# Attention in units of one kv group: 512-column logit matmuls, value products in runs of up to eight key blocks, sums in the values' array form

## The chip, the cores and the metric

The kernel runs on one core of one Trainium2 chip. What is compared is the device time of one launch in microseconds (us). The core has a matrix engine (PE, with its weight loads shown as PEld), a vector engine (DVE), an activation engine (ACT), GpSimd (POOL), and a queue engine (SP) that issues DMA transfers. Each takes its instructions in a fixed order, and they meet at semaphores.

## The reference, cut to what matters

One layer over 4096 tokens of width 1024. An indexer picks up to 256 keys for each query; attention runs over these, with 8 query heads in 2 kv groups of 4 heads, and head width 64. A second branch pools over windows; gates merge both.

```
qg = qb.reshape(B, Q_BLOCK, N_KV_A, rep, HEAD_DIM)        # rep = 4 heads share a kv group
s = jnp.einsum('bqgrd,bqkgd->bqgrk', qg, kg) * scale
s = jnp.where(valid[:, :, None, None, :], s, -jnp.inf)
p = jax.nn.softmax(s, axis=-1)
o = jnp.einsum('bqgrk,bqkgd->bqgrd', p, vg)
...
y = g[:, :, 0] * (a @ w_branch_a[layer]) + g[:, :, 1] * (b @ w_branch_b[layer])
x = x + y @ w_out[layer]
```

The kernel doesn't gather keys. It computes dense causal attention in blocks of 128 queries by 128 keys, and adds a bias of -1e30 to the keys left out.

## The kernel before

Four stages follow one another: the input projection, the indexer with the gates, `phase_attention`, and `phase_out` (the merge and the last projection). In the profiled execution attention begins at about 2110 us and ends at about 3697 us.

`phase_attention` works on query block b = 0..31 in two units, so there are 64. A unit of before holds a "half": two heads of each of the two kv groups. It goes through key blocks kt = 0..b, 1056 in all over the 64 units. The steps of a unit are these.

- `maxima` (L1278 to L1319): for each of its 4 heads the logits with the queries in the partitions (L1296, up to 512 keys a matmul), then a reduction on DVE with the bias (L1302) in pieces of up to 1024 keys, each taking the maximum of the piece before as a scalar from memory. The 4 maxima are turned by a matmul with 4 weight columns (L1311) and written by ACT (L1317) into rows 64 to 67 of `ql`.
- logits again with the keys in the partitions (`logits`, L1337): for each kv group a product of `ks` with `qh` and one of `k2` with `ql` (L1342, L1343), 256 columns each, so four matmuls to a key block, which fill one PSUM bank `st`. DVE adds the turned bias (L1354), and ACT takes the exponential (L1357) into a tile `tt` of two key blocks.
- value products (`values`, L1366): 64 weight columns a group, one group to each half of the array, 256 columns. They are fp32, and each becomes two instructions, so a key block is four instructions. `PVN = 2`: they are issued when two key blocks are there.
- POOL adds up the `tt` tiles (L1382); `sums` (L1396) multiplies the total by 32 columns of ones, in four places of the array. The sums are turned (L1190), inverted on DVE (L1412, L1413), turned again (L1418), copied by ACT (L1420) and stored in `invD`. The unnormalised output goes through `ov` to `oD`.

The rings: `st` has 3 PSUM banks (`SB = 3`) and serves the logits, all transpositions, the turned bias and the sums; `ps` has 2 tiles of two banks for `maxima`; `pv` has one bank. `tt` has 7 tiles, `sm` two.

The order of the instructions is made by `Plan.run`, a model of the engines: each engine takes the ready step of the least key whose new tiles have room. A step is issued whole. The key of a value step is that of its last block plus `LAG`. All DMAs go through SP in that order.

During the last unit the weights of `phase_out` are loaded, `w_branch_a` and then `w_branch_b`, each in 8 pieces of 512 columns through a ring `raw` of two; ACT and DVE split each piece into two parts (L252, L254). `phase_out` starts with branch b.

Of the kernel before, what the change touches and what calls it, by code (L numbers as in the profile page):

```python
# [12 lines left out]
F32 = mybir.dt.float32  # L13
# [13 lines left out]
CH = 512  # L27
# [11 lines left out]
LAG = 6  # L39
SB = 3  # L40
LAT = 0.1
TB = 7
FL = 8
FB = 0
# [19 lines left out]
BS = 0  # L64
# [6 lines left out]
PVN = 2  # L71
# [27 lines left out]
ORDN = 0  # L99


def ORD(n):
    r = list(range(n))
    k = ORDN % 100
    if ORDN < 100:
        return r[k:] + r[:k][::-1]
    if ORDN < 200:
        return r[k:-1] + r[:k][::-1] + r[-1:]
    small, big = r[:k], r[k:]
    out = []  # L110
    while big:
        out.append(big.pop(0))
        if small and len(out) > 2:
            out.append(small.pop())
    return out + small


# [4 lines left out]
class Tile_:  # L122
    """A tile of a plan: its ring, and the steps that use it."""
# [108 lines left out]
class Weights:  # L232
    """The two parts of a matrix [n * P, D], put there by steps of a plan with a ring "raw"."""

    def __init__(self, k, pl, name, n, queue):
        self.k, self.pl, self.name, self.n, self.queue, self.parts, self.steps = k, pl, name, n, queue, [], []

    def put(self, k, key, rows, pool, after=()):
        nc, pl = self.k.nc, self.pl
        for c in range(0, D, CH):  # L240
            raw = pl.new("raw")
            cs = slice(c, c + CH)
# [15 lines left out]
class K:  # L258
# [6 lines left out]
    def consts(self):  # L265
# [13 lines left out]
        self.cst = cp.tile([P, a["cst"].shape[1]], F32, name="cst")  # L279
# [4 lines left out]
    def tables(self, pt):  # L284
        """Small parameters, transposed or spread over the partitions, and the sines and cosines."""
# [50 lines left out]
    def rsqrt(self, pool, v, shape):  # L336
        """v <- 1 / sqrt(v), with one Newton step."""
# [10 lines left out]
    def mm3(self, out, lh, ll, rh, rl, kt):  # L348
        """out = sum over k of (lh + ll)[k]^T (rh + rl)[k] without the product of the two low parts."""
# [6 lines left out]
    def phase1(self):  # L356
# [5 lines left out]
        with ExitStack() as es:  # L362
# [8 lines left out]
            def ep():  # L371
                """The last x is used: its place goes to the first weights and tokens of the next phase."""
# [175 lines left out]
    def on_early(self, part):  # L548
        """What the next phase reads first."""
# [10 lines left out]
    def load_h(self, pool, c, w, bufs):  # L560
        """hi and lo of the transposed normed input, [P, w/128, KT, P], for tokens c*w .. (c+1)*w."""
# [16 lines left out]
    def guess(self, pl, new, ring, key):  # L578
        """A first threshold per row, and how far to look: the scores taken as independent normal heads."""
# [58 lines left out]
    def phase_index(self):  # L638
        """Scores of the indexer, the 256 greatest of each row, and the bias of the keys left out;
        between them the projections of the gates, of z_a and of branch b up to its own projection."""  # L640
# [40 lines left out]
        def span(i):  # L681
            """Time of a slot: the scores of one group and the search of the one before."""
# [13 lines left out]
        # the last tile's key of the indexer  # L696
# [27 lines left out]
        def prep(b, key):  # L724
            """The queries of block b, transposed, four times each: hi, hi, lo, lo."""
# [21 lines left out]
        def scores(b, key, total, free):  # L747
            """The scores of block b, added to what tells equal ones apart."""
# [166 lines left out]
        # the search  # L915
# [21 lines left out]
    def dense(self, pl, new, rp):  # L937
# [19 lines left out]
        def pool(c, g, t, pu, pz, done):  # L957
            """Trailing means of u less u, and silu(z)."""
# [56 lines left out]
        def weight(s, m, kind, i, t):  # L1015
            """The two parts of a block of weights."""
# [131 lines left out]
    def phase_attention(self):  # L1148
        """Attention over the keys that are left. The logits come twice: once with the queries in the
        partitions and the keys in full, the queries' high part, for the maximum of a row, and once with  # L1150
        the keys in the partitions, in full and less that maximum, for the exponentials, which then
        need no transposition before their product with the values."""
        nc, tc, a = self.nc, self.tc, self.a
        self.oD = self.dp.tile([4, P, S], F32, name="oD")
        self.invD = self.dp.tile([8, S], F32, name="invD")
# [4 lines left out]
        v, act, pe = nc.vector, nc.scalar, nc.tensor  # L1160
        ks = sp.tile([P, 2, S], F32R, name="ks")
        k2 = sp.tile([P, 2, S], F32R, name="k2")
# [6 lines left out]
        sel = self.cst[:, 96 + 8 * NB:96 + 8 * NB + 4]  # L1169
# [151 lines left out]
        def softmax(u):  # L1321
# [6 lines left out]
            for kt in range(b + 1):  # L1328
# [8 lines left out]
                def logits(s=s, kt=kt, on=on):  # L1337
                    o = slice(kt * P, (kt + 1) * P)
                    for g in range(2):
# [4 lines left out]
                        if on:  # L1344
                            pe.matmul(out, id4, bc(bt.t[:, kt:kt + 1], [P, 2, P]), start=False, stop=True)
# [282 lines left out]
```

## Time and profile before

| | us |
|---|---|
| median of 3 runs | 4449.38 (4447.02 to 4452.2) |
| span of the profiled execution | 4442.4 |
| attention in it, about | 2110 to 3697 |
| PE busy in the span | 4312.9 (97%) |
| DVE busy in the span | 3328.8 (75%) |
| POOL busy in the span | 1884.9 (42%) |

The median lies 7 us above the span of the profiled execution, which begins at its first instruction and ends at its last. In the page, PE's busy time includes the tail of each matmul, which overlaps the next one; how much room PE has is read from the chain of work that ended last, where each piece has only the time by which it moved the end.

### The profile page before, as it was taken

The numbers are of one execution on the slowest core, as the hardware profiler recorded it, in microseconds if no ns is written. First come the engines' busy times: TensorE is split into PE (matmuls) and PEld (weight loads), VectorE is DVE, ScalarE is ACT, GpSimd is POOL, SyncE is SP. The second block draws the span as 40 slices with busy tenths as digits, with TensorE's granted clock in tenths as the row PEclk, the third lists the DMA queues.
The fourth block names the chain that finished last, engine by engine and source line by source line (L and its number), as shares of the span: only waits on it lengthen the run. The fifth ranks groups of instructions, "written<-read, shape, count | busy, mean of one in ns | idle before, by whom it ended". The sixth has DMA issues, their size and how long they took to land.

```text
span 4442.4 us, 82747 instructions
## 1 busy us (share of the span) xinstructions
PE 4312.9 (97%) x30890; PEld 3656.7 (82%) x30891; DVE 3328.8 (75%) x7933; ACT 2391.8 (54%) x4057; POOL 1884.9 (42%) x1775
## 2 busy tenths in 40 slices
PE   8999999999999999998999999999999998999999
PEld 7998999999998989998666666666666766899998
DVE  5444798999999888896788888888898985343432
ACT  4332786786877778875655555555555553111110
POOL 3555223224334330100356777777777882111111
PEclk9999999999999999999999999999999999999999
DMA  6444445445444456655321111110100005554542
GB/s 204 173 162 155 162 155 183 156 154 183 154 167 153 154 175 200 211 194 175 77 65 40 35 30 32 33 25 27 26 27 19 13 17 169 155 148 137 147 137 86
DMA packets 390912, 523.57 MB, mean 118 GB/s; under 512 B 118189, under 2 KB 294633, under 8 KB 390378
## 3 DMA queue, kind: packets, MB, share of 16 engines
q1 hardware_dynamic: 390506, 518.24, 36.0%
q8 instruction: 244, 4.00, 0.4%
q14 instruction: 162, 1.33, 0.1%
HBM read 374.32 MB, written 143.82 MB: 117 GB/s over the span
## 4 chain that ended last, share of the span: by engine, by line
PE 50%; DVE 1%; DMA 1%; ACT 0%; issue 0%; SPq 0%; POOL 0%; DVEq 0%; ACTq 0%; POOLq 0%
PE pv L1369 12%; PE st L1342 7%; PE ps L1296 6%; PE st L1343 6%; PE po L1522 3%; PE po L1523 3%; PE po L1524 3%; PE pa L1524 3%; PE pa L1523 2%; PE pa L1522 2%; PE st L1190 1%; PE st L1402 1%; PE st L1270 1%; PE st L1311 0%; DMA ga<-gD 0%
## 5 line engine op out<-in xcount | busy, mean ns | idle before, releaser
L1059 PE MATMUL pd<-h,wgh 128*128 128x256 f32 x3584 | 1017.1, 284 | 8.9 <-ACT row L427 8.9
L1382 POOL TENSOR_TENSOR acc<-acc,tt 128x1024 f32<-128x1024 f32 x388 | 925.7, 2386 | 201.7 <-ACT tt L1357 180.6
L1060 PE MATMUL pd<-h,wgh 128*128 128x256 f32 x3584 | 1010.1, 282 | 0.0
L1061 PE MATMUL pd<-h,wgl 128*128 128x256 f32 x3584 | 1009.6, 282 | 0.0
L1357 ACT ACTIVATE tt<-tt 128x512 f32<-128x512 f32 x1056 | 646.3, 628 | 406.5 <-DVE tt L1354 403.2
L1354 DVE TENSOR_TENSOR tt<-st,bT 128x512 f32<-128x512 f32 x1056 | 703.4, 685 | 139.5 <-PE st L1343 127.6
L777 DVE SCALAR_TENSOR_TENSOR ring<-rl,wi,ring 128x1024 f32<-128x1024 f32 (+7 forms) x624 | 699.3, 1161 | 9.3 <-ACT rl L775 6.0
L1059 PEld LDWEIGHTS pd<-h,wgh 128*128 128x128 f32 x3584 | 682.2, 190 | 27.9 <-ACT row L427 9.2
L1060 PEld LDWEIGHTS pd<-h,wgh 128*128 128x128 f32 x3584 | 682.6, 190 | 14.5
L1061 PEld LDWEIGHTS pd<-h,wgl 128*128 128x128 f32 x3584 | 682.0, 190 | 0.0
L775 ACT ACTIVATE rl<-ps 128x1024 f32<-128x1024 f32 (+7 forms) x624 | 538.1, 888 | 133.6 <-PE ps L772 55.0
L1342 PE MATMUL st<-qh,ks 128*128 128x256 f32 x2112 | 593.5, 307 | 4.8 <-DVE tt L1354 2.9
L1369 PE MATMUL pv<-tt,vv 128*64 128x256 f32 x4224 | 573.8, 392 | 0.0
L1343 PE MATMUL st<-ql,k 68*128 68x256 f32 x2112 | 544.0, 283 | 0.4 <-ACT ql L1317 0.4
L1342 PEld LDWEIGHTS st<-qh,ks 128*128 128x128 f32 x2112 | 400.3, 190 | 158.2 <-issue 59.6
L862 ACT ACTIVATE sg<-ring,tk 128x2048 fp8e4<-128x2048 f32 (+8 forms) x322 | 485.4, 1509 | 39.4 <-DVE tk L849 19.6
L1343 PEld LDWEIGHTS st<-ql,k 68*128 68x128 f32 x2112 | 401.4, 190 | 11.5 <-ACT ql L1317 0.7
L1369 PEld LDWEIGHTS pv<-tt,vv 128*64 128x64 f32 x4224 | 255.8, 136 | 179.8 <-issue 49.3
L1302 DVE CUSTOM_DVE_ANT_0 jk<-ps,bias,mx 128x1024 bf16<-128x1024 f32 (+7 forms) x384 | 399.9, 1041 | 2.9 <-PE ps L1296 1.8
L1296 PE MATMUL ps<-ks,qh 128*128 128x512 f32 (+3 forms) x1152 | 372.9, 399 | 2.2 <-DVE mf L1302 1.1
L1555 POOL TENSOR_TENSOR ga<-ga,gb 128x256 f32<-128x256 f32 x128 | 103.9, 821 | 634.4 <-DVE gb L1550 370.9
L772 PE MATMUL ps<-kis,qT 128*128 128x512 f32 (+3 forms) x1136 | 340.1, 388 | 15.0 <-ACT rl L775 14.6
(338 smaller groups left out, 8162.5 us busy)
## 6 DMA issues: line engine op xcount, KB each, us to landing
h<-hD SPq DMA_DIRECT2D x192, 1024.0 KB
gD<-sgm SPq DMA_DIRECT2D x256, 128.0 KB
rowD<-row SPq DMA_DIRECT2D x32, 532.0 KB
x<-x SPq DMA_DIRECT2D x32, 512.0 KB
wraw<-w_in SPq DMA_DIRECT2D x32, 512.0 KB
hD<-hh SPq DMA_DIRECT2D x32, 512.0 KB
hD<-hl SPq DMA_DIRECT2D x32, 512.0 KB
q<-rowD SPq DMA_DIRECT2D x64, 256.0 KB
```

The source lines that it names most:

```text
L775: r = pl.add("act", 0.05 + n * 0.834e-3, k_, lambda ps=ps, rl=rl, n=n: act.activation(rl.t[:, :n], ps.t[:, :n], AF.Relu), [m], use=[ps, rl])
L777: prev[o] = pl.add("dve", 0.1 + n * 1.04e-3, k_, lambda rl=rl, o=o, n=n, h=h: v.scalar_tensor_tensor(acc[:, o:o + n], rl.t[:, :n], self.wi ...
L1059: pe.matmul(out, wh.t[:, k], r1, start=(k == 0), stop=False)
L1060: pe.matmul(out, wh.t[:, k], r2, start=False, stop=False)
L1061: pe.matmul(out, wl.t[:, k], r1, start=False, stop=(k == KT - 1))
L1296: pe.matmul(ps.t[:, s:e], Q[b][0].t[:, h], ks[:, j // 2, o + s:o + e], start=True, stop=True)
L1342: pe.matmul(out, ks[:, g, o], qh.t[:, hs], start=True, stop=False)
L1343: pe.matmul(out, k2[0:68, g, o], ql.t[0:68, hs], start=False, stop=not on)
L1354: ad = pl.add("dve", 0.602, i, lambda s=s, tt=tt, r=r, kt=kt: v.tensor_tensor(tt.t[:, r], s.t, bc(bt.t[:, kt:kt + 1], [P, 4, P]), op=OP.ad ...
L1357: E[kt] = pl.add("act", 0.52, i, lambda tt=tt, r=r: act.activation(tt.t[:, r], tt.t[:, r], AF.Exp), [ad], use=[tt])
L1369: pe.matmul(pv.t[64 * g:64 * g + 64], vv[:, k, 64 * g:64 * g + 64], T[k // 2].t[:, k % 2, 2 * g:2 * g + 2], start=(k == 0), stop=(k == b))
L1382: nc.gpsimd.tensor_tensor(acc.t, first, tt.t, op=OP.add)
```

## The change

A unit is now one kv group g with its four heads.

- Logits: two matmuls of 512 columns to a key block instead of four of 256. `k2` has 65 rows; row 64 is -1, set once by a POOL memset over all 2 x 4096 columns, in place of 32 small POOL copies.
- `maxima`: each piece writes its own column of `mx`, with a constant as the starting scalar; where there are several pieces, a DVE reduction follows. Four transpositions of a column spread over 128 take the place of the 4-column matmul, and one ACT copy of one row takes the place of two.
- Value products: runs of up to 8 key blocks, of even length (`PVN = 8`), `LAG = 4`, 8 `tt` tiles.
- Sums: 64 columns of ones in the two places of the array that the values use, accumulated over both kinds of keys. Turning and inverting is replaced: ACT's copy `sm` (one tile now) is stored to `sumD`, read back as [128, 4], inverted on DVE, and stored to `invD`.
- The weight pieces at the end of attention are of 256 columns, so 16 for each matrix instead of 8, through the same ring of two; `phase_out` has four `raw` tiles of its own, and reads `invD` with four DMAs where it had two.
- Removed: code not in use, and all comments and docstrings.

```diff
-LAG = 6
+LAG = 4
-TB = 7
+TB = 8
-PVN = 2
+PVN = 8
...
-        k2 = sp.tile([P, 2, S], F32R, name="k2")
+        k2 = sp.tile([65, 2, S], F32R, name="k2")
...
-        ones = sp.tile([P, 32], F32, name="ones")
+        ones = sp.tile([P, 64], F32, name="ones")
+        gp.memset(k2[64:65].bitcast(F32), -1.0)
...
-                                               scalar=-3e38 if c == 0 else mx.t[:, c - 1:c], op0=OP.add, op1=OP.max,
-                                               accum_out=mf.t[:, j:j + 1] if c == n_c - 1 else mx.t[:, c:c + 1])
+                                               scalar=-3e38, op0=OP.add, op1=OP.max, accum_out=mx.t[:, j, c:c + 1])
+            if n_c > 1:
+                last = pl.add("dve", 0.12, key, lambda: v.tensor_reduce(
+                    out=mf.t, in_=mx.t[:, :, 0:n_c], op=OP.max, axis=AX.X), [last], [mf], [mx])
+            def turn():
+                for j in range(4):
+                    pe.transpose(pm.t[:, j], bc(mf.t[:, j:j + 1] if n_c > 1 else mx.t[:, j, 0:1], [P, P]), self.ident)
...
-                    for g in range(2):
-                        hs = slice(4 * g + 2 * half, 4 * g + 2 * half + 2)
-                        out = s.t[:, 2 * g:2 * g + 2]
-                        pe.matmul(out, ks[:, g, o], qh.t[:, hs], start=True, stop=False)
-                        pe.matmul(out, k2[0:68, g, o], ql.t[0:68, hs], start=False, stop=not on)
+                    pe.matmul(s.t, ks[:, g, o], qh.t[:, hs], start=True, stop=False)
+                    pe.matmul(s.t, k2[:, g, o], ql.t[0:65, hs], start=False, stop=True)
...
+            runs = -(-(b + 1) // PVN)
+            ends = {-(-(b + 1) * (i + 1) // runs) - 1 for i in range(runs)}
...
             def sums():
+                mine = [(x, r) for x, n in terms for r in range(n)]
+                for x, r in mine:
+                    for f in range(2):
+                        pe.matmul(ps.t[64 * f:64 * f + 64, 0:2], ones, x.t[:, r, 2 * f:2 * f + 2],
+                                  start=((x, r) == mine[0]), stop=((x, r) == mine[-1]))
...
+            s3 = pl.add("dma", 2.0, end + FD, store_sums, [s2], use=[sm])
+            s4 = pl.add("dma", 2.0, end + FD, lambda: sp_dma(rl.t, flat(self.sumD)), [s3], [rl])
+            s5 = pl.add("dve", 0.12, end + FD + FE, lambda: v.reciprocal(rl.t, rl.t), [s4], use=[rl])
+            pl.add("dma", 2.0, end + FD + FE, lambda: sp_dma(flat(self.invD), rl.t), [s5], use=[rl])
...
-        pl.ring("raw", 2, lambda i: self.wp.tile([P, CH], F32, name=f"raw{i}"))
+        pl.ring("raw", 2, lambda i: self.wp.tile([P, CH // 2], F32, name=f"raw{i}"))
```

## Rows read from the trace of the kernel before

**Rows 1.** The span in 40 slices: busy tenths of PE.

```profile
PE   8999999999999999998999999999999998999999
```

**Rows 2.** Busy time by stage: us, then each engine's busy us (and instructions), clock, DMA.

```profile
2110.00:3697.00 1587.00, 1570.94 (x11312) 1082.01 (x11312) 1391.80 (x2572) 872.30 (x1598) 1114.80 (x513) 0.99 0.13 34
...
2266.00:2570.00 304.00, 303.98 (x2209) 207.09 (x2208) 269.44 (x519) 172.41 (x327) 200.74 (x89) 1.00 0.17 41
...
3200.00:3600.00 400.00, 399.70 (x2869) 277.81 (x2868) 359.62 (x628) 211.70 (x370) 314.15 (x135) 1.00 0.07 19
```

**Rows 3.** Chain of work that ended last, 2120 to 3697 us: its shares by line.

```profile
by line: PE pv L1369 33.4%; PE st L1342 20.5%; PE ps L1296 17.4%; PE st L1343 15.8%; PE st L1190 3.3%; PE st L1402 2.6%; PE st L1270 2.0%; PE st L1311 1.2%; DVE tt L1354 0.7%; issue 0.6%; PE st L1418 0.6%; DVE wa L254 0.5%; DVE jk L1302 0.4
```

**Rows 4.** Busy time of L1354 alone by stretch: the count is that of key blocks.

```profile
2266.00:2570.00 304.00, 133.23 (x200) 1.00 0.17 41
2570.00:3000.00 430.00, 197.38 (x296) 1.00 0.12 31
...
3400.00:3600.00 200.00, 93.38 (x142) 1.00 0.03 9
```

**Rows 5.** The chain's pieces in order of time: start, us, what.

```profile
3200.36 1.01 PE pv L1369 x8
3201.37 0.32 PE st L1342
3201.69 0.12 PE st L1343
...
3205.04 0.47 PE ps L1296 x2
3205.51 0.44 PE st L1190 x4
```

**Rows 6.** Longer pieces of the chain: a value run of three blocks, the last sums.

```profile
2171.25 1.45 PE pv L1369 x12
...
3686.64 6.25 PE st L1402 x40
```

**Rows 7.** The chain: sums of one unit; the maxima's turning and what follows it.

```profile
2129.22 0.57 PE st L1402 x8
...
3005.07 0.31 PE st L1311 x2
3005.39 0.66 PE ps L1296 x2
```

**Rows 8.** PE's groups, 2110 to 3697 us: names, shapes, count | busy, mean ns | idle before.

```profile
L1190 PE MATMUL st<-ident,sm 128*128 128x128 f32 x128 | 25.4, 280 | 0.9 <-DVE tt L1354 0.4 <-ACT r L1420 0.4
L1418 PE MATMUL st<-ident,rl 128*4 128x128 f32 x64 | 17.4, 272 | 1.3 <-DVE rl L1413 1.0 <-DVE ql L1252 0.2
```

**Rows 9.** DVE's groups by shape in the same stretch.

```profile
L1354 DVE TENSOR_TENSOR tt<-st,bT 128x512 f32<-128x512 f32 x1056 | 703.4, 685 | 139.5 <-PE st L1343 127.6 <-POOL acc L1382 2.5 <-ACT bT L1273 1.6
L1302 DVE CUSTOM_DVE_ANT_0 jk<-ps,bias,mx 128x1024 bf16<-128x1024 f32 x216 | 275.3, 1275 | 1.4 <-PE ps L1296 1.1
L1302 DVE CUSTOM_DVE_ANT_0 jk<-ps,bias 128x1024 bf16<-128x1024 f32 x200 | 243.1, 1216 | 11.8 <-PE ps L1296 10.9
```

**Rows 10.** The first instructions of attention, in order of time: a POOL memset, PE.

```profile
2110.40 0.29 PE L1270 MATMUL st<-idb,bias 128*128 128x128 bf16 x1 [5.98 <-POOL bias L1238]
...
2110.86 0.31 POOL L1237 MEMSET bias<- 128x256 bf16 x1
...
2114.25 1.94 PE L1190 MATMUL st<-ident,q 128*128 128x128 f32 x8 [1.95 <-DMA q<-rowD]
```

**Rows 11.** The end of attention, in order of time: SP's weight loads, PE's restart.

```profile
3661.57 11.02 SPq L246 DMA_DIRECT2D raw<-w_branch_a  x8
...
3676.74 12.19 SPq L246 DMA_DIRECT2D raw<-w_branch_b  x6
...
3701.15 0.58 PE L1522 MATMUL pa<-bh,wb 128*128 128x256 f32 x1 [6.04 <-ACT bh L1489]
```

**Rows 12.** The chain: a transfer of 256 KB at the end of attention, issue to landing.

```profile
3697.45 3.00 DMA o<-bD
```

More of the change, by code (lines that the diff above doesn't have):

```diff
@@ L63 @@
 ]
-BS = 0
 JK = 2
@@ L96 @@
 HLD = 40.0
[L99 to L115, printed above, removed]
 def bc(ap, shape):
@@ L1190, in transpose2 @@
                 pe.transpose(out.t[:, i], src(i), self.ident)
-        blocks = ORD(NB)
-        units = [(b, half) for b in blocks for half in range(2)]
+        units = [(b, g) for b in range(NB) for g in range(2)]
         at = [0]
@@ L1231, in queries @@
             L = P * (b + 1)
-            bias, q2, qh, ql = new("bs" if b < 8 and BS else "bias"), new("q2"), new("qh"), new("ql")
+            bias, q2, qh, ql = new("bias"), new("q2"), new("qh"), new("ql")
             ld = pl.add("dma", 2.5, base - 8, lambda: twice(q2.t, rows, 0, 8), use=[q2])
@@ L1262, in flip @@
             pt = new("st")
-            key = at[2 * blocks.index(b)] + k0 - BTL
+            key = at[2 * b] + k0 - BTL
             def bank():
@@ L1305, in maxima @@
-                    first = j == 0 and c == 0
-                    last = pl.add("dve", 0.09 + 1.04e-3 * n, key, reduce, [m, last, BI[b][1]],
-                                  [jk] + ([mx] if c == 0 else []) + ([mf] if first else []),
-                                  [ps, BI[b][0]] + ([] if c == 0 else [mx]) + ([] if first else [mf]))
-            pm = new("st")
-            key = at[u] - AL + 0.5
-            t = pl.add("pe", 0.11, key, lambda: pe.matmul(pm.t[64:68, 0], mf.t, self.ident, start=True, stop=True),
-                       [last], [pm], [mf])
@@ L1321, in softmax @@
+            def turn():
+                for j in range(4):
+                    pe.transpose(pm.t[:, j], bc(mf.t[:, j:j + 1] if n_c > 1 else mx.t[:, j, 0:1], [P, P]), self.ident)
+            t = pl.add("pe", 0.44, key, turn, [last], [pm], [mf or mx])
+            M[u] = pl.add("act", 0.49, key, lambda: act.activation(
+                Q[b][1].t[64:65, 4 * g:4 * g + 4], pm.t[64:65], AF.Copy), [t], use=[pm, Q[b][1]])
         def softmax(u):
-            b, half = units[u]
+            b, g = units[u]
@@ L1323, in softmax @@
+            hs = slice(4 * g, 4 * g + 4)
             qh, ql, _ = Q[b]
@@ L1359, in softmax @@
-                if r == 0 and kt < b:
-                    continue
-                some = list(range(done, kt + 1))
-                if len(some) >= PVN or kt == b:
+                    pe.matmul(s.t, ks[:, g, o], qh.t[:, hs], start=True, stop=False)
+                    pe.matmul(s.t, k2[:, g, o], ql.t[0:65, hs], start=False, stop=True)
+                lg = pl.add("pe", 0.455, i, logits, [M[u], K_[kt], last_lg[0] if kt == 0 else None], [s], [qh, ql])
+                last_lg[0] = lg
+                ad = pl.add("dve", 0.602, i, lambda s=s, tt=tt, r=r, kt=kt: v.tensor_tensor(
+                    tt.t[:, r], s.t, bc(bt.t[:, kt:kt + 1], [P, 4, P]), op=OP.add), [lg, turned[kt]],
+                    [tt] if r == 0 else [], [s, bt] + ([tt] if r else []))
@@ L1364, in softmax @@
+                E[kt] = pl.add("act", 0.52, i, lambda tt=tt, r=r: act.activation(tt.t[:, r], tt.t[:, r], AF.Exp),
+                               [ad], use=[tt])
+                if kt in ends:
+                    some = list(range(done, kt + 1))
                     done = kt + 1
@@ L1396, in sums @@
             def sums():
-                for r in range(2):
-                    mine = [x for x, n in terms if r < n] or [T[0]]
-                    for g in range(2):
-                        o = 64 * r + 32 * g
-                        for x in mine:
-                            pe.matmul(ps.t[o:o + 32, 0:2], ones, x.t[:, min(r, b), 2 * g:2 * g + 2],
-                                      start=(x is mine[0]), stop=(x is mine[-1]))
-            s1 = pl.add("pe", 0.5 * len(terms), end + FD, sums, [prev, E[b]], use=[ps] + [x for x, _ in terms])
@@ new lines, in sums @@
+                for x, r in mine:
+                    for f in range(2):
+                        pe.matmul(ps.t[64 * f:64 * f + 64, 0:2], ones, x.t[:, r, 2 * f:2 * f + 2],
+                                  start=((x, r) == mine[0]), stop=((x, r) == mine[-1]))
+            s1 = pl.add("pe", 0.43 * sum(n for _, n in terms), end + FD, sums, [prev, E[b], pvs],
+                        use=[ps] + [x for x, _ in terms])
+            s2 = pl.add("act", 0.27, end + FD, lambda: act.activation(sm.t, ps.t[:, 0:2], AF.Copy), [s1], [sm], [ps])
@@ L1422, in softmax @@
+            pl.add("dma", 2.0, end + FD + FE, lambda: sp_dma(flat(self.invD), rl.t), [s5], use=[rl])
             rows = slice(b * P, (b + 1) * P)
-            pl.add("dma", 2.0, end, lambda: sp_dma(self.invD[4 * half:4 * half + 4, rows], r4.t), [s7], use=[r4])
             def store():
-                for i in range(2):
-                    sp_dma(self.oD[2 * half + i, :, rows], ov.t[:, i])
+                for f in range(2):
+                    sp_dma(self.oD[2 * f:2 * f + 2, 64 * g:64 * g + 64, rows].rearrange("k p c -> p k c"),
+                           ov.t[64 * f:64 * f + 64])
@@ L1431, in phase_attention @@
         first = 0
-        for n, b in enumerate(blocks):
-            base = (at[2 * n - 1] if n else 0) - AL - AP
+        for b in range(NB):
+            base = (at[2 * b - 1] if b else 0) - AL - AP
             while first <= b:
@@ L1594, in cst_array @@
                 c[64 * half:64 * half + 64, 96 + NB * i + b] = x
-    for j in range(4):
-        c[64 + j, 96 + 8 * NB + j // 2] = 1
-        c[64 + j, 98 + 8 * NB + j % 2] = -1
     return c
```

135 lines of the change are left out of this document (53 added, 82 removed).

## The prediction

> **What bounds the kernel now.** I read the slices first, then busy time by stage, then the chain of work that ended last, then its pieces. The slices [rows 1] show PE nearly full everywhere, which alone proves little, as its busy time counts overlapped tails. The table by stage [rows 2] adds the second engine: in attention DVE is busy 1392 of 1587 us, and from 3200 to 3600 us 360 of 400, so 90%. The chain settles it [rows 3]: over the 1577 us of attention almost every piece is PE's, with DVE's additions at 0.7%. So PE's order sets the end, and DVE stands some 10% behind it.
>
> Pace: 200 key blocks in 304 us early, 296 in 430 and 142 in 200 later [rows 4], so 1.52, 1.45 and 1.41 us a block. The query blocks 0 to 7, 8 to 15 and 16 to 31 hold 72, 200 and 784 key blocks; for the last I take 1.43.
>
> **The change part by part.** PE first, by the time a piece adds to the chain.
>
> Value runs. Two key blocks cost 1.01 us [rows 5] and three 1.45 [rows 6], so a block 0.44 and the entry 0.14. The logit matmul behind a run costs 0.32 where its neighbours cost 0.12 [rows 5], so the exit costs 0.20. That is 0.34 us a run. Before, 1056 blocks in pairs make some 530 runs; after, ceil((b+1)/8) a unit makes 160: 8, 16, 24 and 32 blocks at most in one, two, three and four runs, 16 units of each. 370 x 0.34 = 126 us saved: 8 for b up to 7, 23 for 8 to 15, 95 above. A run is one step of the planner, so nothing can break it up.
>
> Logits. Four matmuls of 256 columns cost 4 x 0.12 = 0.48 us; a pair of 512 costs 0.47 [rows 5]. I take 0.014 us a block, 15 us in all, bounds 5 and 25. The Trainium skill ("TensorE: Matmul & The Clock Gate", Back-to-back issue gap) gives columns / 2.4 plus about 2.5 ns at the full clock, so 437 ns against 432: an estimate of 5 us in all for this part. The rows have both shapes some 10% longer than it does, and the sum goes by the rows.
>
> Sums. Eight instructions in four places of the array cost 0.57 us [rows 7], and 0.2 for the exit: 0.77. After, the same eight run two abreast like two value blocks: 2 x 0.44 = 0.87, and 0.34 if no value run stands beside them. That is 0.10 to 0.44 us more a unit; POOL's total comes late, so a place beside a run is not sure, and I take 0.35: +22 us. The last unit's 6.25 us [rows 6] becomes 10 x 0.44 + 0.34 = 4.7: -2.
>
> Turning the sums. Two transpositions and one more fall away in each of 64 units [rows 8]; four cost 0.44 [rows 5], so 0.11 each: -21 us. ACT and DVE steps of this chain are off the path.
>
> Turning the maxima. 0.31 us, and 0.66 for the pair behind it instead of 0.47 [rows 7, 5]: 0.50. After, four transpositions, 0.44, with no change of form: -4 us.
>
> PE's sum is -126 - 15 + 22 - 2 - 21 - 4 = -146 us. For b of 16 and up it is -95 - 11 and about nothing for the rest: 106 of 1121 us, so PE needs 1.43 - 0.135 = 1.295 us a block there.
>
> DVE now. 360 us in 400 at 1.41 us a block [rows 2, 4] is 1.27 us a block. A reduction with a scalar from memory takes 1275 ns, one with a constant 1216 [rows 9]: 59 ns x 384 such pieces = 23 us less. The added reduction takes the place of L1412, one as small. DVE falls to about 1.25 us a block, so it stands only 3 to 4% behind PE, and the buffers between them matter. A run of eight blocks holds PE for 0.14 + 8 x 0.44 + 0.20 = 3.9 us with nothing new for DVE. It can work on up to three `st` banks (3 x 0.69) and two `ps` tiles (2 x 1.2), 4.5 us if all are full. They fill well, as between runs PE makes work faster than DVE does it (0.47 against 0.69 us for logits), but `st` also holds transpositions and turned bias. I charge 0.3 us a run for b of 16 and up (112 runs): +34. Bounds: 0 with full buffers; half full, DVE starves 1.6 us a run, and after 0.3 us of slack that is +150.
>
> For b of 16 and up the sum is -106 + 34 = -72 us. For b from 8 to 15, 23 + 3 + 1 = 27: DVE's 269 of 304 us [rows 2] leave room, -27 us. For b below 8, -9 from the same terms, and against it the stores: SP now carries a round trip for each unit, store, read back, store again, at up to 3.0 us a transfer [rows 12], and its order holds back the loads behind it. In units of 1 to 8 blocks that shows: +9, bounds 0 and 40. Later, loads are 16 block times ahead and hide it; without that cover it is the slower rival below.
>
> Start. The POOL memset over 8192 columns: 256 took 0.31 us [rows 10], so 10 us, ahead of the bias that PE's first instruction waits for. That one moves from 2110.4 to 2120; PE's next wait ended at 2114.25 anyway, so +5 us, bounds 0 and 10.
>
> End. 32 weight pieces go through the ring of two instead of 16. Before, 4 pieces took SP 11.0 us and 6 took 12.2 [rows 11], 2.0 to 2.75 us each with all waits, and PE's restart came after the last ones at 3701. SP's loads of the next stage are queued behind them, and PE waits for those. If a half piece takes half the time this costs 0; if it takes as long, 16 more make +32 to +44. Landing, which doesn't halve, is the larger part: +18 us. The doubled `invD` loads stand beside PE in `phase_out`: 0.
>
> Sum: -72 - 27 + 0 + 5 + 18 - 2 = -78 us. 4442.4 - 78 = 4364 us of span; the median lies 7 us above it: 4371 us.
>
> **The rivals.**
> - PE's whole saving arrives. If all buffers are full when a run begins, DVE's 1.25 us hides under PE's 1.295: the 34 us go, and half of the 18 at the end. About 4328 us. For it: PE and DVE ran without gaps at 90% before. Against: 3% of room.
> - The burst starves DVE, which then is the bound. With 0.8 us a run instead of 0.3 the 112 runs cost 90 us: 4371 - 34 + 90 = 4427 us; half-full buffers all the time, 150, would give 4487. For it: the same 3 `st` banks serve everything. The Trainium skill ("TensorEngine Tiling (Array Packing)", PSUM Bottleneck) says that faster TensorE work leaves the evacuation of PSUM as the bottleneck; the rows agree so far as DVE's 90% goes, and that PSUM's banks then bind no run before shows.
> - Slower: the sums' store. `sm` has one tile, so ACT's copy of a unit's sums waits until SP has stored the one before, and every exponential is queued behind ACT's copy. Where SP stands in a wait for a landing of 3.0 us [rows 12], ACT stands too. The saving of 78 us is gone at 1.2 us for each of 64 units; at 2.5 us, 160 in all, the time is about 4531 us. Against it: a unit of 20 blocks takes 28 us, and a round trip some 9.
> - Nothing moves. The runs are made, but each follows a wait for exponentials that the pairs had hidden: 0.5 us x 160 runs eats the saving, about 4449 us. Against it: `LAG` leaves four blocks, 5 us.
>
> **How the numbers follow.** My forecast, 4371, has 0.58. All of PE's saving has 0.15, a starved DVE 0.16, nothing moved 0.04, slower 0.07. The forecast's own bounds (run starvation 0 to 60, end 0 to 40, small blocks 0 to 40, not all at one end) give 4335 to 4415. The range takes in the first two rivals, 4310 to 4435, and leaves out the last two and the far ends. About 0.2% is what a measurement of this kernel can tell from no change. Faster by more: 0.58 + 0.15 + 0.15 = 0.88; within: 0.05; slower: 0.07.
>
> **What would show it.** In the chain after, value runs of 8 blocks, 32 instructions, at about 3.6 us, some 160 of them, and one long logit piece behind each. Pairs of 512-column logits at 0.47 us. DVE at 93 to 97% between 3000 and 3500 us, and some of the chain now DVE's additions. A pace of 1.33 to 1.35 us a block for b of 16 and up. PE's restart 10 to 30 us behind its last value product. The forecast is wrong if a DVE idle of over 1 us follows each run, if ACT's copy of the sums waits for SP, or if the restart takes over 40 us.

## The result, and the profile after

| | before | after |
|---|---|---|
| median, us, same chip | 4448.38 (4447.02 to 4452.2) | 4473.81 (4471.67 to 4476.05) |
| span of the profiled execution, us | 4442.4 | 4469.9 |

The ratio is 1.0058 (95% interval 1.0044 to 1.0072): slower by 25 us, where 78 us less was forecast, and outside the range of 4310 to 4435 us. Where one execution of a kernel took far longer than its others (8102 and 18901 us in two of the experiments below), it is left out of the median.

To see where the time went, I take the start of the first exponential of each query block (L1357 before, L1325 after) from the traces and add up by groups of query blocks. The tail runs from the end of the last exponential to the end of the span. All in us:

| kernel | first exponential | b 0 to 7 | b 8 to 15 | b 16 to 31 | tail | span |
|---|---|---|---|---|---|---|
| before | 2125.1 | 140.8 | 305.0 | 1115.4 | 756.1 | 4442.4 |
| after | 2124.6 | 172.1 | 304.3 | 1107.3 | 761.7 | 4469.9 |
| forecast for after, minus before | +5 | 0 | -27 | -72 | +16 | -78 |
| measured, minus before | -0.5 | +31.3 | -0.7 | -8.1 | +5.6 | +27.5 |

Three things failed. The large gain in the long query blocks came to a tenth of itself, that of the middle ones did not come, and the short query blocks, forecast at nothing, lost 31 us.

**The long blocks.** After, the busy time by stage has these rows (us of the stretch, then busy us and instructions of PE, PEld, DVE, ACT, POOL, clock, DMA share, GB/s):

```profile
3200.00:3600.00 400.00, 391.60 (x2320) 248.04 (x2317) 349.95 (x633) 214.97 (x354) 314.51 (x136) 1.00 0.07 19
2600.00:3600.00 1000.00, 978.64 (x5836) 623.37 (x5835) 875.15 (x1625) 539.75 (x899) 765.12 (x330) 1.00 0.10 26
```

PE was without a gap in the first of these stretches [rows 2]; now it idles 8 us of 400, and DVE is still at 87%. So neither engine is full. (PE's busy time hides part of what PE loses, as it counts overlapped tails; the chain below shows more.) The additions alone (L1322), by stretch, count key blocks as in [rows 4]:

```profile
2266.00:2570.00 304.00, 129.25 (x196) 0.99 0.23 46
2570.00:3000.00 430.00, 199.43 (x303) 1.00 0.13 30
3400.00:3600.00 200.00, 93.88 (x143) 1.00 0.05 15
```

196, 303 and 143 where before did 200, 296 and 142: the pace hardly moved. The chain of work that ended last, 2600 to 3600 us, by line:

```profile
by line: PE pv L1334 31.3%; PE st L1318 15.2%; PE ps L1274 11.8%; PE st L1319 10.7%; DVE tt L1322 7.3%; issue 7.1%; DVE jk L1280 6.7%; PE st L1367 2.7%; PE st L1249 1.9%; PE st L1172 1.1%; DVE mx L1280 0.9%; PE st L1293 0.6%; DVE ql L1231 0
```

DVE's additions were 0.7% of the chain before and its reductions (`jk`) 0.4% [rows 3]. Now these two hold 14%, and "issue", time between engines that no wait explains, another 7%. A piece of that chain shows where they enter (start us, us, what):

```profile
3466.44 3.60 PE pv L1334 x32
3470.04 0.55 PE st L1249 x8
3470.59 0.53 PE ps L1274 x2
3471.15 0.71 DVE jk L1280
3471.87 0.43 issue
3472.38 0.61 DVE tt L1322
3473.02 0.43 DVE ks L1204
3473.47 0.69 DVE tt L1322
3474.16 1.13 DVE jk L1280
3475.36 0.62 PE ps L1274 x2
...
3478.47 3.17 PE pv L1334 x28
3481.64 0.43 PE st L1318
```

One run of eight key blocks takes 3.60 us, as forecast. From 3471.15 to 3475.36 us the chain is then DVE's. DVE's own order over the same time (start, us, what, and in brackets the idle time before it and what ended it):

```profile
3468.79 0.69 DVE L1322 TENSOR_TENSOR tt<-st,bT 128x512 f32<-128x512 f32 x1
3469.39 0.17 DVE L1381 RECIPROCAL rl<-rl 128x4 f32<-128x4 f32 x1
3471.15 1.23 DVE L1280 CUSTOM_DVE_ANT_0 jk<-ps,bias 128x1024 bf16<-128x1024 f32 x1 [1.59 <-PE ps L1274]
```

At 3469.56, three us into the run, DVE has used up all that stood in PSUM and waits 1.59 us for the next logits. After the run PE has to refill the buffers, and soon waits for DVE to empty them. Over 2600 to 3600 us DVE's two longest groups of waits for PE are these, first before, then after (us in total, times, longest):

```profile
DVE tt L1354 <- PE st L1343: 76.9, 120, 2.0
DVE jk L1302 <- PE ps L1296: 10.7, 21, 0.9
```

```profile
DVE tt L1322 <- PE st L1319: 72.2, 81, 1.9
DVE jk L1280 <- PE ps L1274: 46.1, 43, 2.0
```

The waits of the additions did not grow in total, but became fewer and longer; those of the reductions grew fourfold.

Added up from the trace over the same 1000 us, DVE idles 1.06 us between the start of a value run and 1.5 us after its end; before it was 0.28 us. There are 160 runs in all, as forecast, where before had 533.

**The short blocks.** The sums' matmuls (L1367) of the ninth and tenth unit, and what follows them, look like this:

```profile
2207.73 1.08 PE L1367 MATMUL st<-acc,ones 128*64 128x256 f32 x8
...
2217.23 1.08 PE L1367 MATMUL st<-acc,ones 128*64 128x256 f32 x8 [0.88 <-DVE tt L1322]
2219.84 0.80 PE L1318 MATMUL st<-qh,ks 128*128 128x512 f32 x1 [0.85 <-DVE tt L1322]
2221.10 0.69 DVE L1322 TENSOR_TENSOR tt<-st,bT 128x512 f32<-128x512 f32 x1 [1.23 <-PE st L1319]
2221.84 0.79 PE L1318 MATMUL st<-qh,ks 128*128 128x512 f32 x1 [0.78 <-DVE tt L1322]
2230.70 0.38 ACT L1371 ACTIVATE sm<-st 128x256 f32<-128x256 f32 x1
2231.13 0.50 PE L1318 MATMUL st<-qh,ks 128*128 128x512 f32 x1 [0.96 <-ACT sm L1371]
...
2237.10 0.38 ACT L1371 ACTIVATE sm<-st 128x256 f32<-128x256 f32 x1
```

There are 64 sums and 64 copies, and both come in the order of the units; the copy at 2230.70 is the ninth. So the ninth unit's sums are ready at 2208.8 and copied out at 2230.7, and the tenth's, ready at 2218.3, at 2237.1. From 2217 to 2231 us sums hold two of the three `st` banks, so that the logits go back and forth between PE and DVE through the one that is left: PE waits for DVE to empty it, DVE for PE to fill it. From the start of the sums to the end of ACT's copy, the first nine units hold a bank for 1.1, 30.3, 14.2, 1.9, 12.6, 12.4, 10.4, 11.2 and 23.3 us; before it was 1.1 to 2.3.

### The profile page after: what moved, and what is told of

Its sections match the earlier page's. It is cut to its first block, busy times and chain, and to the rows that moved or that the text cites. A ratio compares the mean times of both kernels' runs of the same rounds, so it can differ in the third digit from the quotient of the medians.

```text
span 4469.9 us, 78672 instructions
## 1 busy us (share of the span) xinstructions
PE 4280.8 (96%) x28706; PEld 3543.3 (79%) x28707; DVE 3297.6 (74%) x7935; ACT 2385.6 (53%) x3945; POOL 1879.9 (42%) x1744
## 5 line engine op out<-in xcount | busy, mean ns | idle before, releaser
L1325 ACT ACTIVATE tt<-tt 128x512 f32<-128x512 f32 x1056 | 654.3, 631 | 577.4 <-DVE tt L1322 571.0
L1322 DVE TENSOR_TENSOR tt<-st,bT 128x512 f32<-128x512 f32 x1056 | 695.4, 683 | 157.6 <-PE st L1319 150.2
L1280 DVE CUSTOM_DVE_ANT_0 jk<-ps,bias 128x1024 bf16<-128x1024 f32 (+7 forms) x640 | 655.0, 1028 | 62.4 <-PE ps L1274 61.3
L1318 PE MATMUL st<-qh,ks 128*128 128x512 f32 x1056 | 479.0, 454 | 23.7 <-DVE tt L1322 15.1
L1334 PE MATMUL pv<-tt,vv 128*64 128x256 f32 x4224 | 497.6, 387 | 0.0
L1334 PEld LDWEIGHTS pv<-tt,vv 128*64 128x64 f32 x4224 | 291.8, 138 | 187.0 <-issue 51.4
L1319 PE MATMUL st<-ql,k 65*128 65x512 f32 x1056 | 421.4, 399 | 0.3 <-ACT ql L1295 0.3
L1318 PEld LDWEIGHTS st<-qh,ks 128*128 128x128 f32 x1056 | 199.7, 189 | 201.2 <-DVE tt L1322 113.3
L1450 ACT ACTIVATE yh<-ga 128x256 fp32r<-128x256 f32 x128 | 53.5, 418 | 516.2 <-PE po L1486 314.8
```

Source lines behind the costliest of these rows:

```text
L1280: v.tensor_tensor_reduce(out=jk.t[:, :n], in0=ps.t[:, :n], in1=BI[b][0].t[:, o:o + n], scale=1.0, scalar=-3e38, op0=OP.add, op1=OP.max, ac ...
L1318: pe.matmul(s.t, ks[:, g, o], qh.t[:, hs], start=True, stop=False)
L1319: pe.matmul(s.t, k2[:, g, o], ql.t[0:65, hs], start=False, stop=True)
L1322: ad = pl.add("dve", 0.602, i, lambda s=s, tt=tt, r=r, kt=kt: v.tensor_tensor(tt.t[:, r], s.t, bc(bt.t[:, kt:kt + 1], [P, 4, P]), op=OP.ad ...
L1325: E[kt] = pl.add("act", 0.52, i, lambda tt=tt, r=r: act.activation(tt.t[:, r], tt.t[:, r], AF.Exp), [ad], use=[tt])
L1334: pe.matmul(pv.t[64 * f:64 * f + 64], vv[:, k, 64 * g:64 * g + 64], T[k // 2].t[:, k % 2, 2 * f:2 * f + 2], start=(k == 0), stop=(k == b))
```

## The experiments

Two theories stood against each other at first: that a run of eight leaves DVE without work, and that the single `sm` tile with its stores holds ACT, and with it the sums' bank. Ratios are to the kernel before, run on the same chip beside it. Stages are those of the table above, "pace" is the time of b 16 to 31 over its 784 key blocks, and idle time of DVE per run is counted as above.

### How long a value run may be, in the new form

> The changed kernel with value runs of up to 4 key blocks instead of 8. Theory A (a run starves DVE): a run of 4 holds PE for 2.1 us, less than the work that waits for DVE in the three st banks and the two ps tiles, so DVE's idle time in a run falls from 1.06 us to 0.3 or less; PE pays 0.34 us for each of about 130 more runs; from 2600 to 3600 us the pace goes from 1.42 to about 1.35 us a key block and the time falls by 40 to 60 us, to about 4425 us. Rival B (PE itself needs 1.42 us a block in the new form): more runs only add 0.34 us each, +40 us, about 4515 us.

```diff
-PVN = 8
+PVN = 4
```

4424.29 us, 0.9951 (0.9933 to 0.9969), as expected. b 16 to 31 took 1060.9 us, a pace of 1.353; b 0 to 7 stayed bad at 171.4. DVE's idle time per run fell to 0.30 us. 2600 to 3600 us, busy by engine and then the chain:

```profile
2600.00:3600.00 1000.00, 999.89 (x6091) 656.05 (x6089) 920.19 (x1694) 558.31 (x938) 804.14 (x345) 1.00 0.10 25
```

```profile
by line: PE pv L1334 34.7%; PE st L1318 21.3%; PE ps L1274 18.1%; PE st L1319 17.3%; PE st L1367 3.2%; PE st L1249 2.4%; PE st L1172 1.7%; PE st L1293 1.4%; issue 0.0%
```

PE has no gap, DVE is gone from the chain, and yet DVE is busier (92%) than with runs of eight. So DVE was not too slow there; it was left without work.

> The changed kernel with value runs of up to 2 key blocks, as before the change. Theory A: PE pays for about 370 more runs at 0.34 us, needs about 1.42 us a key block and is the bound again, the chain from 2600 to 3600 us almost all PE's, DVE's idle time spread over many short waits; about 4465 us, near the changed kernel for another reason. Rival B (PE needs 1.42 with runs of 8): +126 us, about 4600 us.

```diff
-PVN = 8
+PVN = 2
```

4489.92 us, 1.0102 (1.0084 to 1.012), 25 us above what was expected, as the short blocks stayed bad (169.3 us). b 16 to 31 took 1121.4 us, a pace of 1.430, with PE busy 999.6 of 1000 us. PE-bound again, and with all the entries and exits back. That is no faster than before (1115.4): the new logits, sums and turns together gain nothing that shows here.

> The changed kernel without DVE's addition of the bias: the exponential reads the logits' PSUM bank itself, scaled by zero, so the bias and the true exponents are left out and DVE has half its work in attention. Theory A: PE is then the only bound with runs of 8, and shows what it needs: about 1.30 us a key block from 2600 to 3600 us, and about 4350 us in all. Rival B (PE itself is slower than its pieces say): 1.40 us a block or more, 4440 us or more.

The bias is left out, and the exponentials have a scale of zero, so they don't depend on the logits.

```diff
-                ad = pl.add("dve", 0.602, i, lambda s=s, tt=tt, r=r, kt=kt: v.tensor_tensor(
-                    tt.t[:, r], s.t, bc(bt.t[:, kt:kt + 1], [P, 4, P]), op=OP.add), [lg, turned[kt]],
...
-                E[kt] = pl.add("act", 0.52, i, lambda tt=tt, r=r: act.activation(tt.t[:, r], tt.t[:, r], AF.Exp),
+                E[kt] = pl.add("act", 0.52, i, lambda s=s, tt=tt, r=r: act.activation(tt.t[:, r], s.t, AF.Exp, scale=0.0),
...
```

4390.15 us, 0.9876 (0.9855 to 0.9898), 40 us above the total that was expected, as b 0 to 7 took 180.8 us; the pace is what counts here. Busy 2600 to 3600 us, with runs of eight still:

```profile
2600.00:3600.00 1000.00, 999.15 (x6271) 688.86 (x6269) 503.63 (x970) 538.64 (x971) 829.15 (x356) 1.00 0.11 26
```

With DVE at half its work PE has no gap, and the pace is 1025.6 / 784 = 1.308 us. That is PE's own need.

The three fit one sum. For b 16 to 31, runs of 8, 4 and 2 make 112, 208 and 400 runs. At 0.34 us for each run more than 112, PE needs 1.308 + 96 x 0.34 / 784 = 1.350 us a block with fours and 1.308 + 288 x 0.34 / 784 = 1.433 with pairs. Measured: 1.353 and 1.430. Only eights, at 1.412, miss PE's need, by (1.412 - 1.308) x 784 = 82 us, or 0.73 us a run.

### The same number alone, in the kernel before

> The kernel before, with value runs of 8 key blocks and nothing else changed. By its pieces PE saves 0.34 us for each of about 370 runs, 126 us, and would need 1.31 us a key block for query blocks 16 to 31 instead of 1.43. Theory A (a run of 8 starves DVE, in either form): about 1 us of DVE idle time a run comes back, so those blocks gain only 10 to 30 us, and the time is about 4430 us. Rival: only the new form starves DVE; then most of the 126 us arrive, about 4340 us.

> The same kernel as e6 (the kernel before with value runs of 8), for its profile; e6 took 4470 to 4479 us where 4430 was expected, and its profile was of a disturbed execution. Theory A: DVE's idle time per run is 1 us or more, and as the old form needs DVE 1.27 us a key block and not 1.24, blocks 16 to 31 run at 1.44 to 1.46 us a block, slower than with runs of 2. Rival: something else than DVE's starving, such as waits for tt tiles (7 of them, of which a run holds 4), shows in the waits.

Both are this one edit:

```diff
-PVN = 2
+PVN = 8
```

4474.70 us, 1.0067 (1.005 to 1.0084), and 4475.84 us, 1.0066 (1.0045 to 1.0086). Slower than before by some 30 us, where the first expectation had 4430 us: its place was right and its price too low. b 0 to 7 took 142.5 us and b 16 to 31 1137.2, a pace of 1.451, as the second expected. DVE's idle time per run was 1.15 us. The chain of the second, 2600 to 3600 us:

```profile
by line: PE pv L1369 30.4%; PE st L1342 14.4%; PE ps L1296 12.3%; PE st L1343 10.6%; DVE jk L1302 8.5%; DVE tt L1354 7.9%; issue 6.9%; PE st L1270 1.7%; POOL acc L1382 1.4%; PE st L1190 1.3%; PE st L1402 1.2%; PE st L1311 0.7%; ACT r L1420 
```

The same three new entries as in the changed kernel: DVE's two lines and "issue". The starvation needs nothing of the change but its run length; `LAG`, the `tt` tiles and the form of the sums are those of before here. The rival, waits for `tt` tiles that POOL has yet to add up, is there with 1.4% (POOL acc L1382) and can't be the main part.

> The kernel before with value runs of up to 4 key blocks, nothing else changed. If a run of 4 is short enough for the buffers, PE's saving of some 240 runs at 0.34 us arrives in large part: 50 to 70 us, about 4385 us. If the old form gains only in step with the new one's other parts (512-column logits, fewer small steps), 20 us or less, about 4430 us.

```diff
-PVN = 2
+PVN = 4
```

4394.75 us, 0.9884 (0.9867 to 0.99). One number of the kernel before, and 1.2% are there: b 8 to 15 at 296.4 and b 16 to 31 at 1069.3, DVE idle 0.28 us per run. Its chain:

```profile
by line: PE pv L1369 34.6%; PE st L1342 21.3%; PE ps L1296 17.8%; PE st L1343 17.5%; PE st L1190 2.4%; PE st L1270 2.3%; PE st L1402 1.7%; PE st L1311 0.9%; ACT bT L1273 0.5%; PE st L1418 0.3%; DVE tt L1354 0.2%; ACT tt L1357 0.2%; issue 0.
```

### What holds the short blocks

> The changed kernel with two sm tiles instead of one, nothing else. Theory A (held bank): in the changed kernel the sums' st bank stays taken for up to 30 us in the first query blocks, because ACT's copy of the sums waits for the only sm tile to be stored; with two tiles the copy follows the sums in about 1 us, query blocks 0 to 7 take 141 us again instead of 172, and the time falls by some 25 to 35 us, to about 4443 us. Rival (SP queue): it is SP's waits for the reciprocal and the landing that hold back the loads of keys and queries; then blocks 0 to 7 stay at 165 us or more and the time stays within 8 us of 4474.

```diff
-                   "sm": (1, [P, 2, P], F32), "rl": (2, [P, 4], F32)}
+                   "sm": (2, [P, 2, P], F32), "rl": (2, [P, 4], F32)}
```

4482.1 us, 1.0083 (1.0065 to 1.0101). b 0 to 7 took 183.8 us, more than with one tile, and sums still held a bank for up to 31 us among the first nine units. The theory of the single tile falls.

> The changed kernel with the planner's charge for the four transfers at the end of a unit (sums stored, sums read back, inverse stored, output stored) at 0.6 us each instead of 2.0. Only the order of the instructions changes. Two sm tiles changed nothing about the bank that the sums hold. Theory C (the planner): with 8 us of such charges a unit the model's transfer engine is full in the first query blocks, so it puts ACT's copy of the sums far back, and the sums hold one of the three st banks for 10 to 30 us. With the smaller charge the hold falls to some 2 us, query blocks 0 to 7 take 140 to 150 us instead of 172, and the time is about 4447 us. Rival (the round trip itself): SP's real waits for the landing and for the reciprocal hold the loads back; then blocks 0 to 7 stay near 170 us and the time near 4474.

The planner's charge for the four transfers of a unit (store of the sums, reading back, `invD`, `oD`) is lowered. Only the written order changes:

```diff
-            s3 = pl.add("dma", 2.0, end + FD, store_sums, [s2], use=[sm])
-            s4 = pl.add("dma", 2.0, end + FD, lambda: sp_dma(rl.t, flat(self.sumD)), [s3], [rl])
+            s3 = pl.add("dma", 0.6, end + FD, store_sums, [s2], use=[sm])
+            s4 = pl.add("dma", 0.6, end + FD, lambda: sp_dma(rl.t, flat(self.sumD)), [s3], [rl])
...
-            pl.add("dma", 2.0, end, store, [evac], use=[ov])
+            pl.add("dma", 0.6, end, store, [evac], use=[ov])
```

4433.65 us, 0.9976 (0.9966 to 0.9985). b 0 to 7 fell from 172.1 to 145.0 us, and b 8 to 15 from 304.3 to 298.6. A unit that ends at the same time of the span as the one in the rows of after (here the eleventh):

```profile
2218.23 1.08 PE L1367 MATMUL st<-acc,ones 128*64 128x256 f32 x8
2219.73 0.38 ACT L1371 ACTIVATE sm<-st 128x256 f32<-128x256 f32 x1
```

ACT's copy starts 1.5 us behind the start of the sums, where the tenth unit's copy started 19.9 us behind in the rows of after and the ninth's 23.0. SP's waits from 2110 to 2300 us for the inverted sums, after and then here, tell the same (us in total, times, longest):

```profile
SPq L1382 <- DVE rl L1381: 55.1, 11, 8.2
```

```profile
SPq L1382 <- DVE rl L1381: 17.2, 11, 3.4
```

At 2.0 us a transfer the planner's model gives its one transfer engine 8 us a unit, more than a short unit lasts. In the model `sm` then comes free late, and ACT's copy of the next sums is written down late in ACT's order. The transfers, the tiles and the instructions are the same in both kernels, so the wait was one of the written order. The order itself can be counted in the traces: PE's sums of the ninth unit stand behind the logits of the 29th key block in the kernel after and in this one, but ACT's copy of them stands behind the 37th exponential after, and behind the 29th here. (With two `sm` tiles it stood behind the 40th.) Of the first nine units three still hold a bank for longer than 2.4 us: the second for 26, the third for 10, the sixth for 6.

### Both mended

> The changed kernel with both edits: runs of up to 4 key blocks, and the four transfers charged at 0.6 us. If theories A and C are right and independent, the gains add: 47 us for the runs as measured, 25 to 30 us for the first blocks, about 4395 us. If the first blocks are bound by the round trip, about 4424 us as with runs of 4 alone.

The edits of the two experiments, `PVN = 4` and the charge of 0.6, together: 4393.42 us, 0.9885 (0.9865 to 0.9904). b 0 to 7 at 145.5, b 16 to 31 at 1063.6. The two gains add up (the spans fell by 44.7 and 34.6 us singly, by 78.3 together), and the whole equals the kernel before with `PVN = 4`.

### Start and end

> The kernel before, with the last weights of attention loaded in 256-column pieces, 32 instead of 16, through the same ring of two, and nothing else changed. My term for the end was +18 us, with 0 to 40 as bounds. If landing sets the pace of the ring, 10 to 25 us more, about 4462 us; if half a piece takes half the time, no change, 4446 us.

In the kernel before, weight pieces of 256 columns in place of 512 ahead of `phase_out`:

```diff
...
-        self.wa, self.wb = (Weights(self, pl, n, 4, nc.sync) for n in ("wa", "wb"))
+        self.wa, self.wb = (Weights(self, pl, n, 4, nc.sync, CH // 2) for n in ("wa", "wb"))
```

4460.57 us, 1.0037 (1.0023 to 1.0051), so 16.5 us slower; its tail is 775.2, 19 us longer. PE's restart, first here and then in the changed kernel:

```profile
3702.25 0.58 PE L1523 MATMUL pa<-bh,wb 128*128 128x256 f32 x1 [7.58 <-ACT bh L1490]
```

```profile
3729.68 0.58 PE L1485 MATMUL pa<-bh,wb 128*128 128x256 f32 x1 [15.49 <-ACT bh L1450]
```

But the restart waits only 1.5 us more here than in the kernel before [rows 11]. The rest of the 19 us lies behind it, where PE now waits for pieces of `w_branch_b` that ACT has yet to split. PE's waits for them from 3690 us on, first here, then in the changed kernel (the kernel before has none):

```profile
PE pa L1523 <- ACT wb L253: 19.6, 3, 7.2
```

```profile
PE pa L1485 <- ACT wb L231: 9.6, 2, 8.0
```

> As e7 (runs of 4, transfers charged at 0.6 us), and the row of -1 in k2 is written for each key block by a small POOL memset, not by one over 8192 columns. In the changed kernel DVE's first cast lasted 7.0 us beside that memset and PE's first instruction waited 12.7 us. Theory: the first exponential comes some 3 us earlier after attention begins, and the time falls by 2 to 4 us, to about 4391 us. Rival: the first loads set that time anyway; no change.

The mended kernel with the one memset of 8192 columns made into 32 small ones, block by block:

```diff
-        gp.memset(k2[64:65].bitcast(F32), -1.0)
...
+            c = pl.add("pool", 0.3, base - 8, lambda: gp.memset(k2[64:65, :, rows].bitcast(F32), -1.0))
...
```

4389.63 us, 0.9871 (0.9854 to 0.9887), 4 us under the kernel it starts from, though the two intervals overlap. The start, after and then here:

```profile
2105.90 7.01 DVE L1147 CAST idb<-ident 128x128 bf16<-128x128 f32 x1 [4.87 <-DVEq L1067]
2105.91 6.92 POOL L1150 MEMSET k<- 1x8192 f32 x1 [124.70 <-DVEq L1067]
2113.35 0.74 PE L1249 MATMUL st<-idb,bias 128*128 128x128 bf16 x3 [12.71 <-POOL bias L1217]
```

```profile
2108.76 0.40 DVE L1147 CAST idb<-ident 128x128 bf16<-128x128 f32 x1 [4.78 <-DVEq L1067]
2109.59 0.29 PE L1249 MATMUL st<-idb,bias 128*128 128x128 bf16 x1 [6.01 <-POOL bias L1217]
```

> As e11, and the planner is charged what the profile shows: DVE's addition 0.67 us, the exponential 0.63, a reduction of 1024 keys 1.3, the logits 0.47, a value run 0.34 + 0.435 a block. Only the order of instructions changes. If the order made with too cheap a DVE is what leaves 0.05 us a key block over PE's 1.30, blocks 16 to 31 go from 1.36 to about 1.33 us a block, -20 us, about 4370 us. If the buffers set it, no change, about 4391 us.

That kernel with the planner's other charges set to measured durations:

```diff
...
-                    last = pl.add("dve", 0.075 + 1.04e-3 * n, key, reduce, [m, last, BI[b][1]],
+                    last = pl.add("dve", 0.1 + 1.17e-3 * n, key, reduce, [m, last, BI[b][1]],
...
-                ad = pl.add("dve", 0.602, i, lambda s=s, tt=tt, r=r, kt=kt: v.tensor_tensor(
+                ad = pl.add("dve", 0.67, i, lambda s=s, tt=tt, r=r, kt=kt: v.tensor_tensor(
...
-                    pvs = pl.add("pe", 0.235 + 0.428 * len(some), i + LAG, values, [E[k] for k in some] + [pvs],
+                    pvs = pl.add("pe", 0.34 + 0.435 * len(some), i + LAG, values, [E[k] for k in some] + [pvs],
```

4385.56 us, 0.9864 (0.9848 to 0.9881), the best seen, but within the interval of the one before it. Its pace, 1061.0 / 784 = 1.353, is PE's need with runs of four, so the 20 us that the charges might have brought did not come. PE's restart, in a tail of 762.9 us:

```profile
3637.33 0.58 PE L1485 MATMUL pa<-bh,wb 128*128 128x256 f32 x1 [12.72 <-ACT bh L1450]
```

## Why the prediction was wrong

**Value runs on PE: right.** 160 runs, 3.60 us for eight blocks, and 0.34 us for each entry and exit fit all three run lengths. The forecast of PE's need was 1.295 us a block, and without DVE's additions it measured 1.308. That these lie so near is in part luck: the pace of before was taken as 1.43 and is 1.423 (1115.4 / 784). Of 106 us that PE was to save for b 16 to 31, 90 are there (1115.4 - 1025.6), and the runs' part of 95 alone measures 96 (pairs against eights without the additions, 1121.4 - 1025.6).

**DVE's need: right.** From the first exponential of b 16 to the last one, after (DVE's busy time is the third), and the groups of DVE over attention (busy us, mean ns, then idle time before them):

```profile
2601.00:3708.30 1107.30, 1080.23 (x6429) 685.08 (x6429) 968.18 (x1767) 599.59 (x1002) 851.99 (x365) 1.00 0.10 25
```

```profile
L1322 DVE TENSOR_TENSOR tt<-st,bT 128x512 f32<-128x512 f32 x1056 | 695.4, 683 | 157.6 <-PE st L1319 150.2 <-POOL acc L1349 3.8 <-PE ps L1274 2.1
L1280 DVE CUSTOM_DVE_ANT_0 jk<-ps,bias 128x1024 bf16<-128x1024 f32 (+7 forms) x640 | 655.0, 1028 | 62.4 <-PE ps L1274 61.3 <-PE st L1293 0.3
```

DVE's busy time comes to 968.2 / 784 = 1.235 us a block against the forecast 1.25. Its idle time was ended by PE almost always; POOL, which with the value runs frees the `tt` tiles, ended 3.8 us of it.

**The starvation behind a run: the step that failed.** I took 0.3 us a run, with bounds of 0 and 150 us in all, as the value near full buffers. It was 82 us, 0.73 us a run. The row that spoke for full buffers, logits made at 0.47 us and used at 0.69 us, leaves out that PE also makes the `ps` tiles, the turns and the sums between two runs. In the run shown above DVE had 3.1 us of work when it began (3466.44 to 3469.56), not the 4.5 of full buffers. At 1.308 against 1.235 us a block DVE has only 6% of room, and with seven blocks to a run (784 / 112) that is 7 x 0.073 = 0.51 us a run in which it may stand idle at no cost; by this estimate what goes beyond it is lost (1.06 - 0.51 = 0.55, most of the 0.73). The starved rival, at 0.8 us a run, had place and price right, and its chance of 0.16 was too low. The mark set beforehand, "a DVE idle of over 1 us follows each run", is what the trace shows: 1.06. For b 8 to 15 the forecast had no such term, as DVE seemed to have room there. That was wrong too: with the charge at 0.6 us, eights took 298.6 us and fours 291.5, though fours make 24 more runs, 8 us at 0.34. The Trainium skill ("TensorEngine Tiling (Array Packing)", PSUM Bottleneck) says that faster TensorE work may leave the evacuation of PSUM as the bottleneck. Between the runs the trace agrees, as DVE's lines are in the chain. Over the whole it doesn't: DVE was busy 875 of 1000 us with eights and 920 with fours, which were faster. It is when the evacuation gets its work that decided, not how much of it there is.

**Logits, turns and maxima: oversized.** For b 16 to 31, -11 us was forecast for the logits and about nothing for the rest. At equal run length new against old form measured +6 (pairs, 1121.4 against 1115.4) and -6 (fours, 1063.6 against 1069.3): nothing that stands out. The -15 for all blocks rested on 0.48 against 0.47 us, the last digit of a row, and no run separates it from zero. With fours the medians agree too: 4393.42 and 4394.75 us. For b 8 to 15 the forecast was -27. With both edits 13.5 us came (291.5 against 305.0). That is with runs of four, which save 48 runs over pairs here and not 72, so 16 us at 0.34, and 20 with the 4 us for the rest. Some 6 us are missing, and why I can't tell from these runs.

**b 0 to 7: the second step that failed.** The forecast set +9 for the stores, with bounds of 0 and 40, against -9 of savings; +31 was measured, the far end of that bound. I looked for the cost in SP's round trip, and the slower rival in the one `sm` tile. Two tiles did not help, and the transfers did not change when the wait went. The mark set for it, ACT's copy waiting for SP, is not in the trace either: such waits for the stores' landing are 2.4 us in all from 2140 to 2297 us. What cost the time was the planner's own charge: I had read its costs as part of the code and not as something that makes a wait. 27 of the 31 us went with it. That the charge is the cause, and that it moves ACT's copy in the written order, is shown; why the model puts it there is read from the code.

**Start and end.** Start: +5 forecast; the interval from attention's first transfer (2109.2 before, 2105.8 after) to the first exponential grew by 2.9 us, and with the small memsets it is back (15.9 us from 2108.6 to 2124.5, as before). So the cause named is right, at 2.9 us and not 5. The remaining -3.4 us lie ahead of attention, where the change only took out code not in use. End: the term of +18 us for the half pieces is right in size by itself, 16.5 us in the kernel before, though most of it lies in the waits for `w_branch_b` behind the restart and not at the restart. In the changed kernel the tail grew by 5.6 us only: PE's work on attention ends 5.9 us behind the last exponential where it was 8.8 (the forecast had -2 for the sums there), the restart then waits 15.5 us against 6.0 [rows 11], and all behind the restart takes 740.2 us against 741.2, with 9.6 us of waits for `w_branch_b` in it. `phase_out` was changed too (four `raw` tiles), and what that gave back was not separated.

**What stays open.** The 6 us of b 8 to 15, the 26 us for which the second unit's sums hold their bank, and why the restart waits 13 to 15 us in every variant of the changed form with runs of four (tails of 763 to 767 us), against 7 in the old form with fours (759).

## What to carry to other kernels

An uninterrupted stretch on the engine that sets the end should last no longer than the work that lies ready for the next engine, if that engine is within some per cent of being the bound: here 3.2 to 3.6 us lost 0.73 us each time and 1.9 us lost nothing, whatever the engines' totals said. Price such a burst against the buffers as they are when it begins, not as they are when full, and give it the chance that this deserves. And a charge in a planner's model is a part of the kernel like any tile: when a step with several transfers is added, see which shared bank is held in the model's order, and try the smallest edit alone first, since here one number of the old kernel was worth about as much as the whole new form when mended.

## What the runs showed of the hardware

DVE's cast of 128x128 elements from f32 to bf16 took 7.01 us beside POOL's one-partition memset of 6.92 us, and 0.40 us where that memset was cut up (rows of the small memsets above). The two start and end within 0.1 us of each other in the first: the cast ended with POOL's write. Not every POOL instruction does this: in the kernel before, the same cast took 0.23 us though a POOL cast of 0.48 us began with it:

```profile
2109.40 0.48 POOL L1215 CAST k<-cst 4x256 fp32r<-4x256 f32 x1 [124.52 <-DVEq L1088]
2109.40 0.23 DVE L1165 CAST idb<-ident 128x128 bf16<-128x128 f32 x1 [4.58 <-DVEq L1088]
```

The Trainium skill ("SBUF — State Buffer", SBUF: two separate sides) says that DVE, in its modes that use two ports, and GpSimd share a pair of ports, which one instruction holds to its end while the other stands. The rows of the long memset agree with that in length; which of the two held it, and whether the cast ran in such a mode, they don't show. I had priced the memset by itself, at 10 us for 8192 columns from 0.31 us for 256 of another type; it takes 6.92, so a price per column from so short a piece was over 40% too high.
